# One tile shape per burst of small fp32 matmuls, in a two-layer hybrid encoder trunk on one core

## The chip, the cores and the metric

The kernel runs on one core of one Trainium2 chip, as one program. The metric is the device time of that program in microseconds, from repeated runs. The profiled execution is one more run, recorded instruction by instruction. An engine's name is used as in the profile: PE is TensorE's matmul, PEld its weight load, DVE is VectorE, ACT is ScalarE, POOL is GpSimd, SP issues the DMAs.

## What is computed

Two encoder layers over 256 grid tokens and 16 learned meta tokens (272 rows in all) of width 2048, in float32. Each layer, cut to what matters:

```python
proj = h @ w_in            # 6176 columns: GLA q,k,v,gate,decay and NA q,k,v
y_gla = gla_mixer(...)     # 4 heads, dk 128, dv 256, both directions
y_na  = na_mixer(...)      # 16 heads of 64, windows of 4 x 16 tokens plus the meta tokens
h = layer_norm(ALPHA*h + concat(y_gla, y_na) @ w_out)
h = layer_norm(ALPHA*h + square(relu(h @ w_ff1)) @ w_ff2)
```

In the neighbourhood attention (NA) a grid token attends to its window and the 16 meta tokens, with a learned bias; meta tokens attend to meta tokens alone. The gated linear attention (GLA) is, for each head, a matrix of decayed scores between all tokens, times v. The output is the grid tokens' rows, so the second layer needs no meta rows of its queries and outputs (`full` is false there, and rows are 256 instead of 272).

## The kernel before, in words

Activations lie transposed, features on the 128 partitions and tokens along the free axis, each as a pair of fp32r numbers (high and low part). Weights stream from HBM in tiles of 128x1024; ACT makes the high part (`wh`, L147) and DVE the low part (`wl`, L148). Every large product is three fp32r matmuls per 128x128 block, wh*xh, wh*xl, wl*xh (`three`, L151: L160, L161 and L162 for 272 columns, L156 and L157 for 256; `by_k`, L186). These are the stream that PE works through from end to end.

The mixers' work is much smaller and is written as Python generators: one per GLA head (`gla_head`, L436) in a background queue `bg`, one per pair of NA heads (`na_pair`, L584) in a foreground queue `fg`. `by_m` (L190) calls `pump` after every eighth block row, and `pump` takes one step, that is up to the next `yield`, of the head of `fg` and, by a running credit (GLA_R, GLA_NA), of `bg`. So what one step issues stands on PE as a **burst** between two runs of the large matmuls, about 3 us apart. The framework's scheduler decides the last details of the order on each engine. Bursts are plain fp32, which PE runs as two passes with two weight loads; transposes are one pass.

The steps of a GLA head: nine levels (`order`, L480). For each level POOL makes differences of the cumulated decays (L458) in a tile `lev` of two planes, ACT takes exp (L463), DVE multiplies by q and k (L464); then PE makes the 64x64 blocks of scores (L493: four matmuls of 128 rows x 64 columns, in two column halves) or, at level 8, two 128x128 ones (L488). In the first layer, levels 0 to 4 add the meta tokens' own 16x16 block (L496, 16 weight columns). Then come the scores between meta and grid tokens (L518, 16 weight columns and 256 moving ones; L521 in the first layer), the products with v (L536 to L538), the norm and the gate.

The steps of a pair of NA heads:

1. Scores of 128 queries x 176 keys for two token halves and two heads (L595: 64 rows, the head size), bias added by DVE (L598), softmax (L576 to L582).
2. First layer only: the meta queries' scores (L607, 16 weight columns), mask (L608) and softmax.
3. Transposes of v (L613, L614) and copies into v1 and v2 (L617, L620). v2 holds the values of the keys beyond the first 128, both heads in blocks on the diagonal. In the second layer an empty step follows.
4. Transposes of the probabilities (L630, L631), copied by ACT (L632) and DVE (L633).
5. First layer: transpose of the meta probabilities (L637, 16 rows) and its copy (L639). Then the products with the values: for each token half one 128x128 matmul with v2 (L643) and two of 128x64 with v1 (L645), and in the first layer L647 for the meta queries; then the split into y.

Of the kernel before, what the change touches and what calls it, by code (L numbers as in the profile page):

```python
# [19 lines left out]
L = T + NM  # L20
DEPTH = 2
ROWS, GW = 4, 64
GH, GDK, GDV = 4, 128, 256
# [24 lines left out]
class Trunk:  # L48
# [306 lines left out]
            self.nc.vector.tensor_copy(b[:, 0:1], total)  # L355

    def ev_q(self, m, ps):
        self.nc.scalar.mul(self.qk[m][:, 0, :self.n], ps, GDK ** -0.5)

    def ev_k(self, m, ps, **how):  # L360
        self.nc.scalar.activation(self.qk[m][:, 1, :], ps, AF.Identity, **how)

    def ev_v(self, c, ps):
        vt = self.ep.tile([P, L], F32, name="ft", tag="ft", bufs=4)
# [16 lines left out]
    def ev_na(self, j, ps):  # L381

        nc, m = self.nc, j % 3
        src = ps[:, :T].rearrange("p (r t w) -> p t r w", t=2, r=ROWS)
        if m == 0:
            t = self.a2.tile([P, L], F32, name="nq", tag="nq")
            nc.scalar.mul(t[:, :T].rearrange("p (t r w) -> p t r w", t=2, r=ROWS), src, NAD ** -0.5)
            if self.full:
                nc.vector.tensor_scalar(t[:, T:], ps[:, T:], NAD ** -0.5, None, ALU.mult)
            self.nqkv = [t]  # L390
            return
        if m == 1:
            t = self.a2.tile([P, 2, NKEY], F32, name="nk", tag="nk")
            own, rest = t[:, :, :P], t[:, :, P:]
        else:
            t = own, rest = self.nv[j // 3 % 2]
        nc.scalar.copy(own.rearrange("p t (r w) -> p t r w", r=ROWS), src)
        nc.vector.tensor_copy(rest[:, :, 32:NK2], ps[:, None, T:L].to_broadcast([P, 2, NM]))
        grid = lambda a: a.rearrange("p (r w) -> p r w", r=ROWS)
        for h, lo in ((0, 0), (1, 24)):  # L400
            nc.gpsimd.tensor_copy(grid(rest[:, h, :32]), grid(own[:, 1 - h, :])[:, :, lo:lo + 8])
# [34 lines left out]
    def gla_head(self, h):  # L436
# [5 lines left out]
        Am = g2.tile([NM, L], F32, name="Am", tag="Am")  # L442
        level = lambda: g2.tile([P, 2, L], F32, name="lev", tag="lev", bufs=3)

        def operands(lv):
            if lv == 0:
                q2 = level()[:, 0, :]
                nc.gpsimd.tensor_scalar(q2[:, :n], qk[:, 0, :n], 2.0, 0.0, ALU.mult, ALU.add)
                return q2, qk[:, 1, :]
            w = L if full and lv <= 4 else T  # L450
            B, hb = 1 << lv, 1 << (lv - 1)
            nb = w // B
            t = level()
            v = lambda a: a[:, :w].rearrange("p (b h) -> p b h", h=B)
            f, e, tq, tk = v(bf), v(eb), v(t[:, 0, :]), v(t[:, 1, :])
            mf = f[:, :, hb - 1:hb].to_broadcast([P, nb, hb])
            me = e[:, :, hb:hb + 1].to_broadcast([P, nb, hb])
            tt = lambda o, x, y: nc.gpsimd.tensor_tensor(o, x, y, ALU.subtract)  # L458
            tt(tq[:, :, hb:], f[:, :, hb:], mf)
            tt(tq[:, :, :hb], me, e[:, :, :hb])  # L460
            tt(tk[:, :, :hb], mf, f[:, :, :hb])
            tt(tk[:, :, hb:], e[:, :, hb:], me)
            nc.scalar.activation(t[:, :, :w], t[:, :, :w], AF.Exp, scale=1 / TAU)  # L463
            nc.vector.tensor_tensor(t[:, :, :w], t[:, :, :w], qk[:, :, :w], ALU.mult)  # L464
            return t[:, 0, :], t[:, 1, :]

        def across():
            t = level()
            bm, e0 = bf[:, L - 1:L], eb[:, 0:1]
            ts = nc.gpsimd.tensor_scalar  # L470
            ts(t[:, 0, :T], bf[:, :T], bm, 1.0, ALU.subtract, ALU.mult)
            ts(t[:, 1, T:L], bf[:, T:L], bm, -1.0, ALU.subtract, ALU.mult)
            ts(t[:, 0, T:L], eb[:, T:L], e0, -1.0, ALU.subtract, ALU.mult)
            ts(t[:, 1, :T], eb[:, :T], e0, 1.0, ALU.subtract, ALU.mult)
            nc.scalar.activation(t, t, AF.Exp, scale=1 / TAU)
            nc.vector.tensor_tensor(t[:, 0, :n], t[:, 0, :n], qk[:, 0, :n], ALU.mult)
            nc.vector.tensor_tensor(t[:, 1, :], t[:, 1, :], qk[:, 1, :], ALU.mult)
            return t

        order = (7, 0, 1, 2, 3, 4, 5, 6, 8)  # L480
# [1 line left out]
        for at, lv in enumerate(order):  # L482
# [10 lines left out]
                    nc.tensor.matmul(ps[b * 64:b * 64 + 64, s * 64:s * 64 + 64], lhsT=k[:, c:c + 64],  # L493
                                     rhs=q[:, r:r + 64], start=True, stop=True)
            if full and lv <= 4:
                nc.tensor.matmul(ps[:NM, T:L], lhsT=k[:, T:L], rhs=q[:, T:L], start=True, stop=True)  # L496
# [18 lines left out]
            yield  # L515
        t = ahead
        ps = self.bank()
        nc.tensor.matmul(ps[:NM, :T], lhsT=t[:, 1, T:L], rhs=t[:, 0, :T], start=True, stop=True)  # L518
        if full:
            for s in range(2):  # L520
                nc.tensor.matmul(ps[:, T + s * NM:T + s * NM + NM], lhsT=t[:, 1, s * P:s * P + P],  # L521
                                 rhs=t[:, 0, T:L], start=True, stop=True)
# [37 lines left out]
    def na_tiles(self):  # L560

        def t(name, *shape):
            a = self.a2.tile(list(shape), F32, name=name, tag=name, bufs=1)
            self.nc.gpsimd.memset(a, 0.0)
            return a

        self.nv = [(self.a2.tile([P, 2, P], F32, name=f"nv{i}", tag=f"nv{i}", bufs=1), t(f"nr{i}", P, 2, 64))
                   for i in range(2)]
        self.npr = [t(f"npr{i}", P, 4, 64) for i in range(2)]
        self.nv2 = [t(f"nv2{i}", P, 2, P) for i in range(2)]  # L570
        if self.full:
            self.nms = [t(f"nms{i}", NM, 2, 64) for i in range(2)]

    def softmax(self, s, st, u, outs):
        nc = self.nc
# [8 lines left out]
    def na_pair(self, c, q, k, v):  # L584
# [7 lines left out]
        ps = [self.bank() for _ in range(2)]  # L592
        for t in range(2):
            for hh, hs in enumerate(heads):
                nc.tensor.matmul(ps[hh][:, t * NKEY:t * NKEY + NKEY], lhsT=q[hs, t * P:t * P + P], rhs=k[hs, t, :],  # L595
                                 start=True, stop=True)
        for hh in range(2):
            nc.vector.tensor_tensor(s[:, hh:4:2, :], two(ps[hh][:, :2 * NKEY]), bias[:, 2 * hh:2 * hh + 2, :], ALU.add)  # L598
        pr = self.npr[c % 2]
        self.softmax(s, st, 4, ((s[:, :, :P], s[:, :, :P]), (pr[:, :, :NK2], s[:, :, P:])))  # L600
        yield
        if self.full:
            sm = self.nms[c % 2]
            mt = b.tile([NM, 6], F32, name="mst", tag="mst")
            for hh, hs in enumerate(heads):
                ps = self.bank()
                nc.tensor.matmul(ps[:NM, :NK2], lhsT=q[hs, T:L], rhs=k[hs, 0, P:], start=True, stop=True)  # L607
                nc.vector.tensor_tensor(sm[:, hh, :NK2], ps[:NM, :NK2], self.qmask, ALU.add)  # L608
            self.softmax(sm[:, :, :NK2], mt, 2, ((sm[:, :, :NK2],) * 2,))
            yield  # L610
        pv = self.bank()
        for t in range(2):
            nc.tensor.transpose(pv[:, t * P:t * P + P], v[0][:, t, :], self.ident)  # L613
# [6 lines left out]
                nc.vector.tensor_copy(v2[hh * 64:hh * 64 + NK2, t, hs],  # L620
                                      pv[t * 64:t * 64 + NK2, T + hh * NAD:T + hh * NAD + NAD])
        yield
        if not self.full:
            yield
        p1 = b.tile([P, 4, P], F32, name="p1", tag="p1", bufs=1)
        p2 = b.tile([P, 2, P], F32, name="p2", tag="p2", bufs=1)
        for t in range(2):
            pt = self.bank()
            for hh in range(2):
                nc.tensor.transpose(pt[:, hh * P:hh * P + P], s[:, 2 * t + hh, :P], self.ident)  # L630
            nc.tensor.transpose(pt[:, T:T + P], pr[:, 2 * t:2 * t + 2, :].rearrange("p u c -> p (u c)"), self.ident)  # L631
            nc.scalar.copy(p1[:, 2 * t:2 * t + 2, :], two(pt[:, :T]))  # L632
            nc.vector.tensor_copy(p2[:, t, :], pt[:, T:T + P])  # L633
        yield
        if self.full:
            pt = self.bank()
            nc.tensor.transpose(pt[:, :NM], sm.rearrange("p u c -> p (u c)"), self.ident[:NM, :NM])  # L637
            pm = b.tile([P, NM], F32, name="pm", tag="pm")
            nc.vector.tensor_copy(pm, pt[:, :NM])  # L639
        po = self.bank()  # L640
        for t in range(2):
            r = po[:, t * P:t * P + P]
            nc.tensor.matmul(r, lhsT=v2[:, t, :], rhs=p2[:, t, :], start=True, stop=False)  # L643
            for hh, hs in enumerate(heads):
                nc.tensor.matmul(r[hs], lhsT=v1[:, t, hs], rhs=p1[:, 2 * t + hh, :], start=False, stop=True)  # L645
        if self.full:
            nc.tensor.matmul(po[:, T:L], lhsT=v2[:, 0, :], rhs=pm, start=True, stop=True)  # L647
# [365 lines left out]
```

## Time and profile before

| | us |
|---|---|
| median of 3 runs (lowest, highest) | 2437.83 (2437.68, 2437.95) |
| the profiled execution, whole | 2437.55 |
| its span, first to last instruction | 2435.6 |
| PE busy | 2407.7 (99%) |
| PEld busy | 2260.2 (93%) |
| DVE busy | 1574.8 (65%) |
| ACT busy | 1191.6 (49%) |
| POOL busy | 279.9 (11%) |

The granted clock of TensorE is 0.997 of full speed over the span. The DMA engines move 171 GB/s on average and are busy for about half of the time. The mixers of the first layer lie at about 110 to 390 us, those of the second at about 1350 to 1615 us. In a page of the profile, a group of PE rows reads: line, engine, operation, output<-inputs, tile (weight rows*weight columns), moving shape, count. Lengths of matmuls are modelled and overlap; their starts are what can be compared.

### The profile page before, as it was taken

The numbers are of one execution on the slowest core, as the hardware profiler recorded it, in microseconds if no ns is written. First come the engines' busy times: TensorE is split into PE (matmuls) and PEld (weight loads), VectorE is DVE, ScalarE is ACT, GpSimd is POOL, SyncE is SP. The second block draws the span as 40 slices with busy tenths as digits, with TensorE's granted clock in tenths as the row PEclk, the third lists the DMA queues.
The fourth block names the chain that finished last, engine by engine and source line by source line (L and its number), as shares of the span: only waits on it lengthen the run. The fifth ranks groups of instructions, "written<-read, shape, count | busy, mean of one in ns | idle before, by whom it ended". The sixth has DMA issues, their size and how long they took to land.

```text
span 2435.6 us, 43411 instructions
## 1 busy us (share of the span) xinstructions
PE 2407.7 (99%) x17452; PEld 2260.2 (93%) x17452; DVE 1574.8 (65%) x2481; ACT 1191.6 (49%) x1978; POOL 279.9 (11%) x447
## 2 busy tenths in 40 slices
PE   9999999999999999999999999999999999999997
PEld 9999899999999999999999889898988888888886
DVE  6677777785544455546577787778866555666655
ACT  6555555464433344444456555555644333444443
POOL 1164320020000000000020454300200000000000
PEclk9999999999999999999999999999999999999998
DMA  7544444555555555555556445446566566565564
GB/s 239 164 131 149 134 136 156 174 173 174 175 177 176 173 174 175 175 178 174 174 168 185 145 151 152 133 151 198 182 189 187 187 189 190 185 188 189 183 189 130
DMA packets 118361, 417.26 MB, mean 171 GB/s; under 512 B 13388, under 2 KB 16460, under 8 KB 118160
## 3 DMA queue, kind: packets, MB, share of 16 engines
q1 hardware_dynamic: 118160, 414.49, 54.9%
q8 instruction: 137, 2.24, 0.4%
q14 instruction: 64, 0.52, 0.1%
HBM read 412.34 MB, written 2.10 MB: 170 GB/s over the span
## 4 chain that ended last, share of the span: by engine, by line
PE 94%; DVE 2%; POOL 1%; issue 1%; ACT 1%; DMA 0%; SPq 0%; ACTq 0%; POOLq 0%; DVEq 0%
PE mm L156 22%; PE mm L160 17%; PE mm L162 17%; PE mm L161 17%; PE mm L157 11%; PE mm L186 6%; POOL lev L458 1%; PE bg L493 1%; DVE acc L858 1%; DVE wl L148 1%; PE bg L643 0%; PE bg L595 0%; PE bg L645 0%; PE bg L323 0%; PE bg L536 0%
## 5 line engine op out<-in xcount | busy, mean ns | idle before, releaser
L148 DVE TENSOR_TENSOR wl<-raw,wh 128x1024 fp32r<-128x1024 f32 (+1 forms) x772 | 946.0, 1226 | 648.9 <-ACT wh L147 640.5
L147 ACT CAST wh<-raw 128x1024 fp32r<-128x1024 f32 (+1 forms) x772 | 805.5, 1044 | 951.4 <-PE mm L161 405.5
L160 PE MATMUL mm<-x,wh 128*128 128x272 f32 (+2 forms) x2176 | 632.7, 291 | 0.0
L161 PE MATMUL mm<-x,wh 128*128 128x272 f32 (+2 forms) x2176 | 627.8, 288 | 0.0
L162 PE MATMUL mm<-x,wl 128*128 128x272 f32 (+2 forms) x2176 | 627.6, 288 | 0.0
L160 PEld LDWEIGHTS mm<-x,wh 128*128 128x128 f32 x2176 | 412.5, 190 | 4.4 <-issue 1.4
L162 PEld LDWEIGHTS mm<-x,wl 128*128 128x128 f32 x2176 | 410.2, 188 | 0.2
L161 PEld LDWEIGHTS mm<-x,wh 128*128 128x128 f32 x2176 | 409.6, 188 | 0.0
L156 PE MATMUL mm<-x,wh 128*128 128x512 f32 x1152 | 409.4, 397 | 0.0
L157 PE MATMUL mm<-x,wl 128*128 128x256 f32 x1152 | 324.5, 282 | 0.1
L156 PEld LDWEIGHTS mm<-x,wh 128*128 128x128 f32 x1152 | 217.5, 189 | 52.0 <-issue 1.2
L156 PE MATMUL mm<-y,wh 128*128 128x512 f32 x704 | 247.9, 393 | 0.0
L157 PEld LDWEIGHTS mm<-x,wl 128*128 128x128 f32 x1152 | 217.3, 189 | 0.5 <-DVE wl L148 0.4
L162 PE MATMUL mm<-y,wl 128*128 128x272 f32 x704 | 203.1, 288 | 0.0
L160 PE MATMUL mm<-y,wh 128*128 128x272 f32 x704 | 203.1, 288 | 0.0
L161 PE MATMUL mm<-y,wh 128*128 128x272 f32 x704 | 202.7, 288 | 0.0
L157 PE MATMUL mm<-y,wl 128*128 128x256 f32 x704 | 197.5, 281 | 0.5 <-DVE wl L148 0.5
L156 PE MATMUL mm<-u,wh 128*128 128x512 f32 x512 | 180.6, 393 | 0.0
L458 POOL TENSOR_TENSOR lev<-be 128x128 f32<-128x128 f32 (+1 forms) x256 | 154.7, 634 | 121.7 <-PE bg L493 30.5
L156 PEld LDWEIGHTS mm<-y,wh 128*128 128x128 f32 x704 | 131.8, 187 | 29.9
L162 PE MATMUL mm<-u,wl 128*128 128x272 f32 x512 | 147.7, 289 | 0.0
L160 PE MATMUL mm<-u,wh 128*128 128x272 f32 x512 | 147.7, 288 | 0.0
(242 smaller groups left out, 3286.7 us busy)
## 6 DMA issues: line engine op xcount, KB each, us to landing
raw<-in_wff SPq DMA_DIRECT2D x512, 512.0 KB, 3.5
raw<-in_win SPq DMA_DIRECT2D x190, 512.0 KB, 3.6
raw<-in_wout SPq DMA_DIRECT2D x64, 512.0 KB, 3.6
nb<-in_nab SPq DMA_DIRECT2D x16, 352.0 KB, 3.4
out<-acc SPq DMA_DIRECT2D x8, 256.0 KB, 2.2
xraw<-in_xT SPq DMA_DIRECT2D x7, 272.0 KB, 5.5
wraw<-in_wup SPq DMA_DIRECT2D x2, 392.0 KB
raw<-in_win SPq DMA_DIRECT2D x4, 128.0 KB, 3.0
```

What stands on the lines that cost most here:

```text
L147: nc.scalar.copy(wh[:, c], raw[:, c])
L148: self.wl = nc.vector.tensor_tensor(wl[:, c], raw[:, c], wh[:, c].bitcast(F32), ALU.subtract).ins
L156: mm(ps, lhsT=wh[:, c:c + P], rhs=x.both[:, :, :T], start=first, stop=False)
L157: mm(ps[:, T:], lhsT=wl[:, c:c + P], rhs=xh[:, :T], start=False, stop=last)
L160: mm(o, lhsT=wh[:, c:c + P], rhs=xh[:, :n], start=first, stop=False)
L161: mm(o, lhsT=wh[:, c:c + P], rhs=xl[:, :n], start=False, stop=False)
L162: mm(o, lhsT=wl[:, c:c + P], rhs=xh[:, :n], start=False, stop=last)
L186: self.nc.tensor.matmul(ps[m][:, :n], lhsT=parts[p][0][:, c:c + P], rhs=acts[j][parts[p][1]][:, :n], start=j + p == 0, stop=j == nk - 1 an ...
L458: tt = lambda o, x, y: nc.gpsimd.tensor_tensor(o, x, y, ALU.subtract)
L493: nc.tensor.matmul(ps[b * 64:b * 64 + 64, s * 64:s * 64 + 64], lhsT=k[:, c:c + 64], rhs=q[:, r:r + 64], start=True, stop=True)
L858: return self.nc.vector.tensor_tensor(v, v, by[:, None, :].to_broadcast([P, m, n]), alu)
```

## The change

Within a burst, neighbouring matmuls get the same tile shape (rows and columns of the stationary operand):

- Probabilities times values: the 128x128 matmul with v2 becomes two of 128x64, one per head, in the shape of those with v1; the meta queries' product (L647) too.
- L496: 64 weight columns instead of 16 (the 48 more are whatever lies behind, and their results are not read). For this k is plane 0 and q plane 1 of each two-plane tile, so that the columns behind k's last 16 exist.
- L518: 128 weight columns instead of 16, in the same way.
- L607: the meta queries' scores move into step 1, behind L595, with 128 weight columns instead of 16 (so the meta columns stand first in the query tile); their results lie in the same banks as the others, and the mask is added there.
- L637: the transpose of the meta probabilities becomes a full 128x128 one and moves into step 4 (its tile has 128 rows, zeros below the meta rows), with its copy.
- The empty step of the second layer now comes ahead of the transposes of v; the first layer's number of steps stays.

```diff
     def ev_q(self, m, ps):
-        self.nc.scalar.mul(self.qk[m][:, 0, :self.n], ps, GDK ** -0.5)
+        self.nc.scalar.mul(self.qk[m][:, 1, :self.n], ps, GDK ** -0.5)
...
             if full and lv <= 4:
-                nc.tensor.matmul(ps[:NM, T:L], lhsT=k[:, T:L], rhs=q[:, T:L], start=True, stop=True)
+                nc.tensor.matmul(ps[:64, T:L], lhsT=k[:, T:T + 64], rhs=q[:, T:L], start=True, stop=True)
...
-        nc.tensor.matmul(ps[:NM, :T], lhsT=t[:, 1, T:L], rhs=t[:, 0, :T], start=True, stop=True)
+        nc.tensor.matmul(ps[:, :T], lhsT=flat(t)[:, T:T + P], rhs=t[:, 1, :T], start=True, stop=True)
...
-            self.nms = [t(f"nms{i}", NM, 2, 64) for i in range(2)]
+            self.nms = [t(f"nms{i}", P, 2, 64) for i in range(2)]
...
-                nc.tensor.matmul(ps[hh][:, t * NKEY:t * NKEY + NKEY], lhsT=q[hs, t * P:t * P + P], rhs=k[hs, t, :],
+                nc.tensor.matmul(ps[hh][:, t * NKEY:t * NKEY + NKEY], lhsT=q[hs, NM + t * P:NM + t * P + P], rhs=k[hs, t, :],
                                  start=True, stop=True)
+        if self.full:
+            for hh, hs in enumerate(heads):
+                nc.tensor.matmul(ps[hh][:, 2 * NKEY:2 * NKEY + NK2], lhsT=q[hs, :P], rhs=k[hs, 0, P:],
+                                 start=True, stop=True)
+            meta = self.nms[c % 2]
+            sm = meta[:NM, :, :NK2]
         for hh in range(2):
             nc.vector.tensor_tensor(s[:, hh:4:2, :], two(ps[hh][:, :2 * NKEY]), bias[:, 2 * hh:2 * hh + 2, :], ALU.add)
+            if self.full:
+                nc.vector.tensor_tensor(sm[:, hh, :], ps[hh][:NM, 2 * NKEY:2 * NKEY + NK2], self.qmask, ALU.add)
...
         if self.full:
-            sm = self.nms[c % 2]
             mt = b.tile([NM, 6], F32, name="mst", tag="mst")
-            for hh, hs in enumerate(heads):
-                ps = self.bank()
-                nc.tensor.matmul(ps[:NM, :NK2], lhsT=q[hs, T:L], rhs=k[hs, 0, P:], start=True, stop=True)
-                nc.vector.tensor_tensor(sm[:, hh, :NK2], ps[:NM, :NK2], self.qmask, ALU.add)
-            self.softmax(sm[:, :, :NK2], mt, 2, ((sm[:, :, :NK2],) * 2,))
-            yield
+            self.softmax(sm, mt, 2, ((sm, sm),))
+        yield
         pv = self.bank()
...
         yield
-        if not self.full:
-            yield
         p1 = b.tile([P, 4, P], F32, name="p1", tag="p1", bufs=1)
...
             nc.tensor.transpose(pt[:, T:T + P], pr[:, 2 * t:2 * t + 2, :].rearrange("p u c -> p (u c)"), self.ident)
+            if self.full and t:
+                nc.tensor.transpose(pt[:, T + P:], meta.rearrange("p u c -> p (u c)"), self.ident)
             nc.scalar.copy(p1[:, 2 * t:2 * t + 2, :], two(pt[:, :T]))
             nc.vector.tensor_copy(p2[:, t, :], pt[:, T:T + P])
-        yield
         if self.full:
-            pt = self.bank()
-            nc.tensor.transpose(pt[:, :NM], sm.rearrange("p u c -> p (u c)"), self.ident[:NM, :NM])
             pm = b.tile([P, NM], F32, name="pm", tag="pm")
-            nc.vector.tensor_copy(pm, pt[:, :NM])
+            nc.vector.tensor_copy(pm, pt[:, T + P:T + P + NM])
+        yield
         po = self.bank()
         for t in range(2):
             r = po[:, t * P:t * P + P]
-            nc.tensor.matmul(r, lhsT=v2[:, t, :], rhs=p2[:, t, :], start=True, stop=False)
-            for hh, hs in enumerate(heads):
-                nc.tensor.matmul(r[hs], lhsT=v1[:, t, hs], rhs=p1[:, 2 * t + hh, :], start=False, stop=True)
+            for rest in (True, False):
+                for hh, hs in enumerate(heads):
+                    nc.tensor.matmul(r[hs], lhsT=(v2 if rest else v1)[:, t, hs],
+                                     rhs=p2[:, t, :] if rest else p1[:, 2 * t + hh, :],
+                                     start=rest, stop=not rest)
         if self.full:
-            nc.tensor.matmul(po[:, T:L], lhsT=v2[:, 0, :], rhs=pm, start=True, stop=True)
+            for hs in heads:
+                nc.tensor.matmul(po[hs, T:L], lhsT=v2[:, 0, hs], rhs=pm, start=True, stop=True)
```

`flat` lays the two planes of a tile end to end. In the changed kernel the lines are numbered anew: L493 becomes L497, L496 L500, L518 L522, L521 L525, L595 L599, L607 L603, L613 L620, L630 and L631 L635 and L636, L637 L638, L643 and L645 both L650, L647 L655.

More of the change, by code (lines that the diff above doesn't have):

```diff
@@ L357, in ev_q @@
     def ev_q(self, m, ps):
-        self.nc.scalar.mul(self.qk[m][:, 0, :self.n], ps, GDK ** -0.5)
+        self.nc.scalar.mul(self.qk[m][:, 1, :self.n], ps, GDK ** -0.5)
     def ev_k(self, m, ps, **how):
-        self.nc.scalar.activation(self.qk[m][:, 1, :], ps, AF.Identity, **how)
+        self.nc.scalar.activation(self.qk[m][:, 0, :], ps, AF.Identity, **how)
     def ev_v(self, c, ps):
@@ L386, in ev_na @@
             t = self.a2.tile([P, L], F32, name="nq", tag="nq")
-            nc.scalar.mul(t[:, :T].rearrange("p (t r w) -> p t r w", t=2, r=ROWS), src, NAD ** -0.5)
+            nc.scalar.mul(t[:, NM:].rearrange("p (t r w) -> p t r w", t=2, r=ROWS), src, NAD ** -0.5)
             if self.full:
-                nc.vector.tensor_scalar(t[:, T:], ps[:, T:], NAD ** -0.5, None, ALU.mult)
+                nc.vector.tensor_scalar(t[:, :NM], ps[:, T:], NAD ** -0.5, None, ALU.mult)
             self.nqkv = [t]
@@ L443, in gla_head, with flat @@
         level = lambda: g2.tile([P, 2, L], F32, name="lev", tag="lev", bufs=3)
+        def flat(t):
+            return t.rearrange("p a c -> p (a c)")
         def operands(lv):
             if lv == 0:
-                q2 = level()[:, 0, :]
-                nc.gpsimd.tensor_scalar(q2[:, :n], qk[:, 0, :n], 2.0, 0.0, ALU.mult, ALU.add)
-                return q2, qk[:, 1, :]
+                q2 = level()[:, 1, :]
+                nc.gpsimd.tensor_scalar(q2[:, :n], qk[:, 1, :n], 2.0, 0.0, ALU.mult, ALU.add)
+                return q2, flat(qk)
             w = L if full and lv <= 4 else T
@@ L454, in operands @@
             v = lambda a: a[:, :w].rearrange("p (b h) -> p b h", h=B)
-            f, e, tq, tk = v(bf), v(eb), v(t[:, 0, :]), v(t[:, 1, :])
+            f, e, tq, tk = v(bf), v(eb), v(t[:, 1, :]), v(t[:, 0, :])
             mf = f[:, :, hb - 1:hb].to_broadcast([P, nb, hb])
@@ L464, in operands @@
             nc.vector.tensor_tensor(t[:, :, :w], t[:, :, :w], qk[:, :, :w], ALU.mult)
-            return t[:, 0, :], t[:, 1, :]
+            return t[:, 1, :], flat(t)
         def across():
@@ L470, in across @@
             ts = nc.gpsimd.tensor_scalar
[L471 to L474, printed above, removed]
+            ts(t[:, 1, :T], bf[:, :T], bm, 1.0, ALU.subtract, ALU.mult)
+            ts(t[:, 0, T:L], bf[:, T:L], bm, -1.0, ALU.subtract, ALU.mult)
+            ts(t[:, 1, T:L], eb[:, T:L], e0, -1.0, ALU.subtract, ALU.mult)
+            ts(t[:, 0, :T], eb[:, :T], e0, 1.0, ALU.subtract, ALU.mult)
             nc.scalar.activation(t, t, AF.Exp, scale=1 / TAU)
-            nc.vector.tensor_tensor(t[:, 0, :n], t[:, 0, :n], qk[:, 0, :n], ALU.mult)
-            nc.vector.tensor_tensor(t[:, 1, :], t[:, 1, :], qk[:, 1, :], ALU.mult)
+            nc.vector.tensor_tensor(t[:, 1, :n], t[:, 1, :n], qk[:, 1, :n], ALU.mult)
+            nc.vector.tensor_tensor(t[:, 0, :], t[:, 0, :], qk[:, 0, :], ALU.mult)
             return t
@@ L517, in gla_head @@
         ps = self.bank()
-        nc.tensor.matmul(ps[:NM, :T], lhsT=t[:, 1, T:L], rhs=t[:, 0, :T], start=True, stop=True)
+        nc.tensor.matmul(ps[:, :T], lhsT=flat(t)[:, T:T + P], rhs=t[:, 1, :T], start=True, stop=True)
         if full:
             for s in range(2):
-                nc.tensor.matmul(ps[:, T + s * NM:T + s * NM + NM], lhsT=t[:, 1, s * P:s * P + P],
-                                 rhs=t[:, 0, T:L], start=True, stop=True)
+                nc.tensor.matmul(ps[:, T + s * NM:T + s * NM + NM], lhsT=t[:, 0, s * P:s * P + P],
+                                 rhs=t[:, 1, T:L], start=True, stop=True)
             nc.vector.tensor_copy(A[:, 2:6:3, :NM], ps[:, T:T + 2 * NM].rearrange("p (s c) -> p s c", s=2))
@@ L631, in na_pair @@
             nc.tensor.transpose(pt[:, T:T + P], pr[:, 2 * t:2 * t + 2, :].rearrange("p u c -> p (u c)"), self.ident)
+            if self.full and t:
+                nc.tensor.transpose(pt[:, T + P:], meta.rearrange("p u c -> p (u c)"), self.ident)
             nc.scalar.copy(p1[:, 2 * t:2 * t + 2, :], two(pt[:, :T]))
             nc.vector.tensor_copy(p2[:, t, :], pt[:, T:T + P])
+        if self.full:
+            pm = b.tile([P, NM], F32, name="pm", tag="pm")
+            nc.vector.tensor_copy(pm, pt[:, T + P:T + P + NM])
         yield
-        if self.full:
-            pt = self.bank()
-            nc.tensor.transpose(pt[:, :NM], sm.rearrange("p u c -> p (u c)"), self.ident[:NM, :NM])
-            pm = b.tile([P, NM], F32, name="pm", tag="pm")
-            nc.vector.tensor_copy(pm, pt[:, :NM])
         po = self.bank()
```

## The prediction

> **What bounds the kernel now.** First the page's chain of work that ended last, by engine:
>
> ```profile
> PE 94%; DVE 2%; POOL 1%; issue 1%; ACT 1%; DMA 0%; SPq 0%; ACTq 0%; POOLq 0%; DVEq 0%
> ```
>
> TensorE is the bound: 94% of the chain is its own work. A microsecond taken from PE's queue is a microsecond off the end, except where something else feeds the chain. So I priced the mixers' bursts, the small fp32 products that stand between the big fp32r ones (L156 to L162, called main matmuls here). The timeline of PE, cut to four places, shows one of each sort; columns are start, length, engine, line, tile rows*columns, moving shape, count.
>
> ```profile
> 115.12 0.29 PE L162 MATMUL mm<-x,wl 128*128 128x272 f32 x1
> 115.34 0.45 PE L493 MATMUL bg<-lev 128*64 128x64 f32 x8
> 115.72 0.39 PE L160 MATMUL mm<-x,wh 128*128 128x272 f32 x1
> 115.95 0.29 PE L161 MATMUL mm<-x,wh 128*128 128x272 f32 x1
> ```
> ```profile
> 219.81 0.29 PE L162 MATMUL mm<-x,wl 128*128 128x272 f32 x1
> 219.94 0.38 PE L630 MATMUL bg<-ident,ns 128*128 128x128 f32 x2
> ...
> 220.51 0.37 PE L160 MATMUL mm<-x,wh 128*128 128x272 f32 x1
> 220.72 0.29 PE L161 MATMUL mm<-x,wh 128*128 128x272 f32 x1
> ```
> ```profile
> 223.49 0.29 PE L162 MATMUL mm<-x,wl 128*128 128x272 f32 x1
> 223.70 0.45 PE L493 MATMUL bg<-lev 128*64 128x64 f32 x8
> 224.09 0.23 PE L637 MATMUL bg<-ident,nms 16*128 16x16 f32 x1
> 224.25 0.49 PE L643 MATMUL bg<-p,nv 128*128 128x128 f32 x2
> 224.66 0.44 PE L645 MATMUL bg<-p,v 128*64 128x128 f32 x4
> 225.03 0.49 PE L643 MATMUL bg<-p,nv 128*128 128x128 f32 x2
> 225.45 0.44 PE L645 MATMUL bg<-p,v 128*64 128x128 f32 x4
> 225.82 0.40 PE L647 MATMUL bg<-pm,nv 128*128 128x16 f32 x2
> 226.15 0.45 PE L493 MATMUL bg<-lev,qk 128*64 128x64 f32 x8
> 226.53 0.22 PE L496 MATMUL bg<-lev,qk 128*16 128x16 f32 x2
> 226.67 0.39 PE L160 MATMUL mm<-x,wh 128*128 128x272 f32 x1
> 226.90 0.29 PE L161 MATMUL mm<-x,wh 128*128 128x272 f32 x1
> ```
>
> Starts are to be read, since lengths overlap. A main matmul of 272 columns follows its neighbour at 0.125 us. The burst's **price** is start to start, from the main matmul ahead to the second one behind, less two ordinary steps (0.25 us). The four transposes-only rows (128*128, six records at 0.108) cost 220.72 - 219.81 - 0.25 = 0.66 us: nothing but their own 6 x 0.11. The level products (128*64) cost 0.58, of which their streams are four pairs at 0.053 (the records' starts: 0, 0.007, 0.106, 0.113, 0.165, ...: two column halves run side by side) = 0.21; so **a stay in another shape costs about 0.36** for going in, the first weight load and coming out. Every change of shape between two rows of the third timeline costs again.
>
> An fp32 stream of 128 columns takes 0.107 us, by L643's records (second pass 0.108 behind the first where its weights were already in). For the pair L645 the second pass starts 0.161 behind the first = 0.053 weight load + 0.107, so both halves of 128 columns were through in 0.107.
>
> **The change part by part.** Prices below are no-wait prices of such bursts in the trace, worked out as above.
>
> (1) Probabilities times values, 16 pairs of heads. Before, the two token halves take 0.42 + 0.37 each (224.25 to 225.82: 1.57 for eight streams of 0.107 = 0.86). After, L643 becomes two 128x64 matmuls side by side, same streaming, no change of shape: 0.86 + 0.36 = 1.22. Layer 1 (no meta products): price before 1.575 (at 1591.84), so 8 x 0.355 = 2.8. Layer 0: price before with L637 and L647 is 2.16; after, L647 as two 64-column products adds between 0 (hidden) and 0.24 (the two passes' rows of L647: 0.132 + 0.112); two pair loads of 0.053 less the shorter way out make 0.08, nearest to the L493 rows. 2.16 - 1.30 = 0.86, x 8 = 6.9.
>
> (2) Where levels and these products share a burst they now have one shape. Layer 1's L645 to L493 already shows it: 0.103 from start to start against 0.203 from L645 to L643. Two bursts of layer 0 cost 2.64 before and 1.30 + 0.21 = 1.51 after, 0.27 beyond (1); the burst above costs 3.16, and its parts, now split, 1.57 + 0.58: 0.16 beyond. Sum 0.7.
>
> (3) L496, 20 of them: adding one to a burst costs 0.147 now (0.725 against 0.58). Widened to 64 columns it needs no new shape: two loads of 0.053, less 0.046 because 16 columns leave sooner (L496 goes out in 0.106, L493 in 0.152) = 0.06; bounds 0 and 0.147. 17 x 0.09 = 1.5. Three stand between two levels, where the second level then needs no new entry: 1.248 - 0.725 = 0.52 against 0.23 + 0.06, 3 x 0.23 = 0.7. Sum 2.2.
>
> (4) L518, 8 of them: price 0.735. As 128*128 fp32 it streams as long (2 x 0.215; L536's 256-column rows give 0.215 a pass) plus 0.02, as L488's four 128-column passes cost 0.45 in all. 8 x 0.285 = 2.3. Widening the weights from 16 to 128 columns costs nothing while a 0.107 load lies under a 0.215 stream.
>
> (5) L607: alone 0.39 three times, in company 0.18 to 0.38; sum 2.3. In L595's burst, after: a hidden load, a load of 0.107 in view, less a shorter exit, 0.15 each, between 0.05 (streams alone, 48/128 of 0.107) and 0.21 (two loads); 8 x 0.15 = 1.2. Gain 1.1.
>
> (6) L637 becomes a full transpose in the transposes' burst: 8 x 0.109 = 0.9 lost.
>
> The other edits (index order of the pairs, the query's meta columns first) keep sizes and counts on DVE, ACT and POOL; the mask additions only move ahead of the softmax (0.19 us each). The step that waits on the softmax is still 9 us of main matmuls behind it, so they are hidden; uncovered they would be 16 x 0.19 = 3 us. In layer 1 the transposes of v and its copies (L617 0.36, four of L620 at 0.23) go one step, about 3 us, later; they stay ahead of the p step. No DMA is added, and the wait of POOL for L496 falls away with it.
>
> Sum: 2.8 + 6.9 + 0.7 + 2.2 + 2.3 + 1.1 - 0.9 = **15.1 us** of PE, 4.0 of it in layer 1 (2.8, and half of 2.3).
>
> What comes back as waits: in the chain of layer 1's mixers (1350 to 1615 us) POOL's L458 holds 8.1% and issue 4.6%, and PE's own waits there are
>
> ```profile
> PE bg L493 <- DVE lev L464: 1.6, 2, 1.3
> PE bg L643 <- DVE p L633: 0.8, 1, 0.8
> ```
>
> so a quarter of that stretch isn't PE's: I take 1.0 of the 4.0 back. In layer 0's mixers PE's listed waits sum to 0.2 us; I take back 0.4. Net 15.1 - 1.4 = 13.7. The profiled execution took 2437.55 (span 2435.6 and 1.95 around it); 2437.55 - 13.7 = 2423.85, and the median of the runs lies 0.28 above that execution: **2424.1**. Behind the mixers PE is nearly gapless to the end and DMA half idle, so nothing there eats the gain.
>
> The Trainium skill, TensorEngine Tiling, Key Properties, states that a change of tiling mode drains TensorE while a change of tile doesn't. The trace agrees for the fp32 products (0.203 against 0.103 above), but not everywhere: L323's fp32r products alternate 64 and 32 columns at the main matmuls' own 0.125.
>
> **The rivals.**
> A. Weight loads of one burst don't lie under its streams: then a pass pair of 128 columns takes 0.16 rather than 0.107, 16 x 8 x 0.053 = 6.8 us are lost, and 2430.9 comes out. For it: no row of before has more than two such pass pairs in a row. Against: in L645 the second loads start 0.054 after the first, during the first stream, and in L493 four loads lie under streams.
> The Trainium skill, TensorE: Matmul & The Clock Gate, Part 3, has the rule that would do this: loads overlap running matmuls only in another row group, and the halves share theirs. Those L493 records speak against it.
> B. The halves of a long burst run one after the other: each of the 8 pass pairs takes 0.107 more, 16 x 0.86 = 13.7, which eats the gain: 2437.8. Against: L645's 0.161.
> C. The gain is absorbed: layer 1's 4.0 wholly, and 2 of layer 0's 11.1, where ACT is busy for 50 to 55% and DVE for 66 to 77% (busy time by window): 15.1 - 6.0 = 9.1, 2428.7. For it: the POOL chain. Against: PE's few waits.
> D. Slower: L650 comes sooner after the copies of p and takes the wait that the drains hid. The longest such wait is 1.06 us (at 1544, L643 for L633). The place is the head of all 16 bursts; from 13.7/16 = 0.86 us each the change loses; at 1.06 each, 2437.8 - 13.7 + 17.0 = 2441.1. Against: 13 of 16 have no such wait now, and between the p step and this one lie 2.7 to 3 us of main matmuls in both kernels.
> E. The change does not do what it says, since the entry and exit belong to fp32 in narrow shapes whatever stands beside them: only the widening is left, 0.9 + 0.4 + 20 x 0.06 less L637's own 0.3, about +2: 2440. Against: L645 to L493 at 0.103.
>
> **How the numbers follow.** Forecast 0.76 (bounds of the unknown terms, 20 x 0.08 + 8 x 0.16 + 8 x 0.1, about 3.5 either way: 2420.6 to 2427.6), A 0.08, C 0.07, B 0.03, D 0.03, E 0.03. The range goes from 2420.5 to 2431, so as to take in C and A; what is outside is B, D, E and the forecast's own misses. A measurement of this kernel tells about 0.2% (4.9 us) from no change. Faster by more: forecast, A, C = 0.91; within: B, E and a little of D = 0.07; slower: 0.02.
>
> **What would show it.** Right: bursts of L650 that read x16 or more in 128*64 without another shape between, price near 1.2 to 1.3; L522 entered 0.13 after a main matmul; L500 at 0.05 behind L497. Wrong: pass pairs of L650 0.16 or 0.21 apart (A, B); idle time at L650 that ends with DVE or ACT (D); PE's busy time down by 15 while the span falls by less than 10 (C). A span above 2430 means that one of these terms is mis-sized.

## The result and the profile after

The changed kernel takes 2424.98 us (median of 4 runs, 2424.90 to 2425.17) against 2437.76 (2437.33 to 2437.95): 12.8 us less, ratio 0.9948 with a 95% interval of 0.9931 to 0.9965. The forecast was 2424.1, in a range of 2420.5 to 2431. The page of the profiled execution (2424.98 us) begins, with the chain's shares by engine as the last line:

```profile
span 2423.2 us, 43590 instructions
...
PE 2392.5 (99%) x17532; PEld 2259.4 (93%) x17532; DVE 1575.1 (65%) x2481; ACT 1191.2 (49%) x1978; POOL 290.6 (12%) x447
...
PE 93%; DVE 3%; POOL 1%; issue 1%; ACT 1%; DMA 0%; SPq 0%; ACTq 0%; POOLq 0%; DVEq 0%
```

PE executes 80 records more and is busy for 15.2 us less; the other engines execute as many instructions as before (POOL's spans are rough). The span is 12.4 us shorter. The timeline of PE after shows the values' burst that the prediction showed between 223.49 and 226.90 us:

```profile
223.21 0.29 PE L162 MATMUL mm<-x,wl 128*128 128x272 f32 x1
223.49 0.44 PE L650 MATMUL bg<-p,nv 128*64 128x128 f32 x4
223.76 0.39 PE L650 MATMUL bg<-p,v 128*64 128x128 f32 x4
223.97 0.39 PE L650 MATMUL bg<-p,nv 128*64 128x128 f32 x4
224.19 0.39 PE L650 MATMUL bg<-p,v 128*64 128x128 f32 x4
224.41 0.24 PE L655 MATMUL bg<-pm,nv 128*64 128x16 f32 x4
224.50 0.43 PE L497 MATMUL bg<-lev,qk 128*64 128x64 f32 x8
224.76 0.24 PE L500 MATMUL bg<-lev,qk 128*64 128x16 f32 x2
224.93 0.39 PE L160 MATMUL mm<-x,wh 128*128 128x272 f32 x1
225.16 0.29 PE L161 MATMUL mm<-x,wh 128*128 128x272 f32 x1
```

Everything stands in 128*64. Each L650 row is two pass pairs; in the burst the pairs start 0.109 us apart, the time of one stream of 128 columns, so both column halves stream side by side. The burst now costs 225.16 - 223.21 - 0.25 = 1.70 us; with the one level that now stands in the burst ahead (0.58) that makes 2.28, where it was 3.16. (The transpose L637, now L638, went to that burst too, and adds 0.11 there.)

Where the time went is seen best by following the same main matmuls through both traces. Between two fixed ones around layer 0's mixers the stretch took 292.0 us before (102.5 to 394.5) and 284.7 after: 7.4 us less. Around layer 1's it took 288.0 (1340.1 to 1628.1) and 283.2: 4.75 less. Ahead of the two, the changed kernel is 0.4 us later; between them nothing changed, and behind them it gains 0.4. The prediction had 10.7 and 3.0. So the total came close partly because two misses have opposite signs, and PE's waits say where to look. A row names the engine and line that waited and what released it, then us in total, times and the longest. In layer 0's mixers the list had one row before, and has five after:

```profile
PE bg L647 <- DVE pm L639: 0.2, 1, 0.2
```
```profile
PE bg L540 <- ACT Am L528: 1.3, 1, 1.3
PE bg L650 <- DVE p L640: 0.6, 1, 0.6
PE bg L522 <- DVE lev L481: 0.4, 1, 0.4
PE bg L635 <- DVE nv L627: 0.3, 1, 0.3
PE bg L635 <- DVE ns L586: 0.2, 1, 0.2
```

In layer 1's mixers three rows of the list are new, and L643's row of 0.8 us, shown in the prediction, has no successor:

```profile
PE mm L157 <- DVE wl L148: 0.4, 1, 0.4
PE bg L635 <- DVE nv L627: 0.3, 1, 0.3
PE bg L635 <- DVE ns L586: 0.2, 1, 0.2
```

### The profile page after: what moved, and what is told of

Read it like the earlier page. It is cut to its first block, busy times and chain, and to the rows that moved or that the text cites. A ratio compares the mean times of both kernels' runs of the same rounds, so it can differ in the third digit from the quotient of the medians.

```text
span 2423.2 us, 43590 instructions
## 1 busy us (share of the span) xinstructions
PE 2392.5 (99%) x17532; PEld 2259.4 (93%) x17532; DVE 1575.1 (65%) x2481; ACT 1191.2 (49%) x1978; POOL 290.6 (12%) x447
## 4 chain that ended last, share of the span: by engine, by line
PE 93%; DVE 3%; POOL 1%; issue 1%; ACT 1%; DMA 0%; SPq 0%; ACTq 0%; POOLq 0%; DVEq 0%
PE mm L156 22%; PE mm L160 17%; PE mm L162 17%; PE mm L161 17%; PE mm L157 11%; PE mm L186 5%; POOL lev L462 1%; DVE wl L148 1%; PE bg L497 1%; DVE acc L866 1%; PE bg L650 1%; PE bg L599 0%; PE bg L540 0%; PE bg L323 0%; PE bg L541 0%
## 5 line engine op out<-in xcount | busy, mean ns | idle before, releaser
L148 DVE TENSOR_TENSOR wl<-raw,wh 128x1024 fp32r<-128x1024 f32 (+1 forms) x772 | 946.9, 1227 | 656.0 <-ACT wh L147 646.4
L462 POOL TENSOR_TENSOR lev<-be 128x128 f32<-128x128 f32 (+1 forms) x256 | 162.1, 663 | 108.2 <-ACT gt L337 26.9
```

Of the source, the lines that this page charges most:

```text
L148: self.wl = nc.vector.tensor_tensor(wl[:, c], raw[:, c], wh[:, c].bitcast(F32), ALU.subtract).ins
```

## The experiments

Theory 1 going in: a burst's price depends on its shapes alone, so parts add up; the new waits come from the order that the scheduler now chose on ACT, POOL and DVE. Theory 2: layer 0's helper engines can't follow a faster PE, so part of any gain there comes back as waits.

| kernel | median, us | ratio to before (interval) | layer 0, us less | layer 1, us less |
|---|---|---|---|---|
| changed | 2424.98 | 0.9948 (0.9931 to 0.9965) | 7.4 | 4.75 |
| pv_only | 2428.47 | 0.9964 (0.9951 to 0.9977) | 4.7 | 4.1 |
| gla_only | 2435.15 | 0.9992 (0.9982 to 1.0002) | 1.7 | 0.5 |
| meta_only | 2434.77 | 0.9990 (0.9981 to 1.0000) | 1.0 | 1.4 |
| serial_halves | 2425.02 | 0.9950 (0.9935 to 0.9965) | 7.3 | 4.3 |
| near_shapes | 2427.57 | 0.9962 (0.9948 to 0.9976) | 5.0 | 4.1 |
| am_first | 2423.26 | 0.9944 (0.9929 to 0.9959) | 8.9 | 4.7 |
| level7_wide | 2424.35 | 0.9949 (0.9934 to 0.9963) | 8.3 | 4.3 |
| am_level7 | 2422.63 | 0.9941 (0.9926 to 0.9956) | 9.9 | 4.3 |
| light_dve | 2422.46 | 0.9939 (0.9924 to 0.9954) | 8.8 | 5.6 |
| early_v | 2425.33 | 0.9951 (0.9934 to 0.9967) | 7.4 | 4.5 |
| changed, again | 2424.81 | 0.9948 (0.9933 to 0.9963) | 7.35 | 4.8 |

The kernel before took 2437.08 beside the second to fifth, 2436.93 beside the four with a shape or an order changed (near_shapes to am_level7), and 2437.18 beside the last three. The two right columns are taken from one trace each, between the same main matmuls as above; the two traces of the changed kernel agree within 0.05. By their ratios gla_only and meta_only can't be told from the kernel before, nor most of the lower rows from the changed one, so what follows on them rests on the traces.

### The three parts alone

pv_only makes this edit to the kernel before:

```diff
-            nc.tensor.matmul(r, lhsT=v2[:, t, :], rhs=p2[:, t, :], start=True, stop=False)
-            for hh, hs in enumerate(heads):
-                nc.tensor.matmul(r[hs], lhsT=v1[:, t, hs], rhs=p1[:, 2 * t + hh, :], start=False, stop=True)
+            for rest in (True, False):
+                for hh, hs in enumerate(heads):
+                    nc.tensor.matmul(r[hs], lhsT=(v2 if rest else v1)[:, t, hs],
+                                     rhs=p2[:, t, :] if rest else p1[:, 2 * t + hh, :],
+                                     start=rest, stop=not rest)
...
-            nc.tensor.matmul(po[:, T:L], lhsT=v2[:, 0, :], rhs=pm, start=True, stop=True)
+            for hs in heads:
+                nc.tensor.matmul(po[hs, T:L], lhsT=v2[:, 0, hs], rhs=pm, start=True, stop=True)
```

> The kernel before with one edit: probabilities times values as 128x64 pairs (L643, L645 and L647 in one shape); everything else, L637 ahead of them too, stays. Theory 1 (a price per burst that depends on shapes alone, so that parts add up): the burst costs 1.22 us in layer 1 instead of 1.575 and 1.45 to 1.47 in layer 0 instead of 2.16, as L637's own shape still costs its 0.16 there; 8 x 0.355 + 8 x 0.70 = 8.4 us, some 0.5 more where levels share the burst, less up to 1 us of new waits: 2428.3 to 2430. Theory 2 (layer 0's helpers cannot follow a faster PE, so about a third of any gain in layer 0 comes back as waits, in proportion to the gain): 2.8 + 4.0, about 2431, with waits of PE spread over the bursts of layer 0.

gla_only takes from the change the lines of `ev_q`, `ev_k` and `gla_head`:

```diff
-                nc.tensor.matmul(ps[:NM, T:L], lhsT=k[:, T:L], rhs=q[:, T:L], start=True, stop=True)
+                nc.tensor.matmul(ps[:64, T:L], lhsT=k[:, T:T + 64], rhs=q[:, T:L], start=True, stop=True)
...
-        nc.tensor.matmul(ps[:NM, :T], lhsT=t[:, 1, T:L], rhs=t[:, 0, :T], start=True, stop=True)
+        nc.tensor.matmul(ps[:, :T], lhsT=flat(t)[:, T:T + P], rhs=t[:, 1, :T], start=True, stop=True)
```

> The kernel before with the GLA part alone: planes of q and k swapped, L496 with 64 and L518 with 128 weight columns. Theory 1: 17 x 0.075 + 3 x 0.25 + 8 x 0.29 = 4.3 us less PE work, 3.1 of it in layer 0; waits of its own from a changed order on ACT and POOL, or none, whichever way the order falls: 2433.5 to 2434.5. Theory 2: a third of layer 0's 3.1 comes back: 2434.5, again with waits in proportion to what is saved.

meta_only takes the rest: L607 and L637 moved and widened, the empty step moved, with the values' products as before.

```diff
+        if self.full:
+            for hh, hs in enumerate(heads):
+                nc.tensor.matmul(ps[hh][:, 2 * NKEY:2 * NKEY + NK2], lhsT=q[hs, :P], rhs=k[hs, 0, P:],
+                                 start=True, stop=True)
...
+            if self.full and t:
+                nc.tensor.transpose(pt[:, T + P:], meta.rearrange("p u c -> p (u c)"), self.ident)
```

> The kernel before with the meta tokens' moves of the NA part alone: L607 moved behind L595 and widened, L637 a full transpose in the transposes' burst, the empty step of layer 1 moved; probabilities times values in the old shapes. Theory 1: L607's 2.3 us less 8 x 0.15, less 8 x 0.11 for the transposes, and 8 x 0.35 as L643 is entered from a main matmul in its own shape once L637 is gone: 3.0 us, all in layer 0: 2434.8. Theory 2: 2435.8. If moving the meta work alone brings the late copies of Am in front of L536 (a wait of about 1.3 us once in the changed kernel), the order made by this part is the cause of that wait.

The prices came as theory 1 had them: the values' burst at 1.22 us in layer 1 and 1.455 in layer 0 with L637 still ahead; L500 adds 0.07. In pv_only the time is as theory 1 expected too, though PE has new waits for the copy of the meta probabilities there:

```profile
PE bg L650 <- DVE pm L639: 1.1, 2, 0.9
```

gla_only is a miss for both theories: 1.9 us gained (2437.08 to 2435.15) where 2.6 at the least had been expected. In layer 0 its bursts are 3.0 us cheaper (1.8 by L500, 1.2 by L522), 1.7 arrived. At 141 us the wait for the levels' DVE product (L481) takes what the cheaper L518 gave: start to start, 0.41 became 0.71 there. Most of the rest stands at 246 us (0.4), where PE waits for the copies of p and pm, and at 315 (0.2). In layer 1 the four cheaper L522 make 1.2 us, and 0.5 arrived. meta_only's time (2434.77) is what theory 1 said (2434.8), but by luck: the 3.0 us were to come in layer 0, and 1.0 came there and 1.4 in layer 1. It shows waits at 265, 287, 314 and 380 us, the places where the changed kernel has four of its five; at L536 the listed wait is 0.4, not 1.3, so this part's order makes at most some of that one. The layer 0 gains of the three parts add up to the whole (4.7 + 1.7 + 1.0 = 7.4). Those of layer 1 do not (4.1 + 0.5 + 1.4 = 6.0 against 4.75): two parts each take away the same wait, see early_v.

### Is it the shape around them?

near_shapes gives both widened GLA products a width next to that of the shape around them:

```diff
-                nc.tensor.matmul(ps[:64, T:L], lhsT=k[:, T:T + 64], rhs=q[:, T:L], start=True, stop=True)
+                nc.tensor.matmul(ps[:32, T:L], lhsT=k[:, T:T + 32], rhs=q[:, T:L], start=True, stop=True)
...
-        nc.tensor.matmul(ps[:, :T], lhsT=flat(t)[:, T:T + P], rhs=t[:, 1, :T], start=True, stop=True)
+        nc.tensor.matmul(ps[:64, :T], lhsT=flat(t)[:, T:T + 64], rhs=t[:, 1, :T], start=True, stop=True)
```

> The changed kernel with its two widened GLA products made narrower than the shape around them: L500 with 32 weight columns instead of 64, L522 with 64 instead of 128. Theory 1 (only the same tile shape saves the entry and exit): L500 adds 0.15 again instead of 0.07, 20 times, with 0.17 more for each of three pairs in one burst, and L522 costs 0.74 alone instead of 0.45, 8 times: 1.5 + 0.5 + 2.3 = 4.3 us more, some of it where PE waits anyway: 2428 to 2429.3. Rival (it was the very narrow 16 columns that cost, whatever stands around them): 2425.0.

The timeline of PE, first of the changed kernel, then of near_shapes, at the same burst:

```profile
119.28 0.45 PE L497 MATMUL bg<-lev,qk 128*64 128x64 f32 x8
119.56 0.24 PE L500 MATMUL bg<-lev,qk 128*64 128x16 f32 x2
119.73 0.39 PE L160 MATMUL mm<-x,wh 128*128 128x272 f32 x1
```
```profile
119.02 0.45 PE L497 MATMUL bg<-lev,qk 128*64 128x64 f32 x8
119.40 0.23 PE L500 MATMUL bg<-lev,qk 128*32 128x16 f32 x2
119.57 0.39 PE L160 MATMUL mm<-x,wh 128*128 128x272 f32 x1
```

With 64 columns L500 starts 0.28 behind the levels' first matmul and the burst is left 0.45 after its start; with 32 columns, half the weights, it starts 0.38 behind and the burst lasts 0.55. Burst by burst, L500 adds 0.17 instead of 0.07, and L522 alone costs 0.78 instead of 0.44. So it is the same shape that saves, not a less narrow one; rival E of the prediction falls with it. (The time, 2427.57, is a little under theory 1's 2428 to 2429.3.) The Trainium skill, TensorEngine Tiling, Key Properties, has this as the drain at a change of tiling mode, and this run agrees: 0.152 from the last L497 to L500 in another shape, 0.024 to 0.059 in the same one.

The sum is as telling: these prices make 5.2 us, but only 3.0 arrived (2.35 in layer 0, 0.65 in layer 1). The bursts at 142 and 310 us, which waits make 0.67 and 0.69 us longer in the changed kernel, are 0.07 and 0.08 longer here: PE work put back in filled the waits.

### Must the halves be neighbours?

serial_halves turns two loops of the changed kernel round:

```diff
-            for rest in (True, False):
-                for hh, hs in enumerate(heads):
+            for hh, hs in enumerate(heads):
+                for rest in (True, False):
```

> The changed kernel with one edit: in probabilities times values all products of the first head come before those of the second, so that neighbours stand in the same column half. Theory 1 (two matmuls of 64 columns run side by side only as neighbours in different halves): each of the 16 bursts takes 8 passes of 0.107 more, 0.86 us, 13.7 in all: about 2438.7. Rival (TensorE finds the pairs whatever their order, or what the change saved is not in side by side running): about 2425, the same as the changed kernel.

The rival was right. The burst on PE's timeline:

```profile
287.66 0.29 PE L162 MATMUL mm<-x,wl 128*128 128x272 f32 x1
287.88 0.45 PE L650 MATMUL bg<-p,nv 128*64 128x128 f32 x4
288.15 0.39 PE L650 MATMUL bg<-p,v 128*64 128x128 f32 x4
288.36 0.44 PE L650 MATMUL bg<-p,nv 128*64 128x128 f32 x4
288.58 0.44 PE L650 MATMUL bg<-p,v 128*64 128x128 f32 x4
288.80 0.29 PE L655 MATMUL bg<-pm,nv 128*64 128x16 f32 x4
289.02 0.39 PE L160 MATMUL mm<-x,wh 128*128 128x272 f32 x1
289.25 0.29 PE L161 MATMUL mm<-x,wh 128*128 128x272 f32 x1
```

From the main matmul ahead to the second one behind it takes 1.59 us, where the changed kernel's takes 1.55 at the same burst. Record by record, the second head's first matmul, which the program has behind four passes of the first head, starts 0.013 us after the first head's first; then both halves go on with a pass each 0.109. In the second token half they run 0.057 apart, where the changed kernel has 0.006.

### The wait at 262 us: order or pace?

am_first pins one order of the changed kernel:

```diff
-        nc.scalar.copy(Am[:, :T], ps[:NM, :T])
+        self.am = nc.scalar.copy(Am[:, :T], ps[:NM, :T]).ins
...
-            nc.scalar.activation(t[:, :, :w], t[:, :, :w], AF.Exp, scale=1 / TAU)
+            with self.tc.issue_after(self.am) if self.am else ExitStack():
+                nc.scalar.activation(t[:, :, :w], t[:, :, :w], AF.Exp, scale=1 / TAU)
```

> The changed kernel with one order fixed: from the first head's copy of Am (L528) on, ACT's exp of a level is issued behind the Am copy that was traced before it. In the changed kernel PE waits 1.4 us once, at 262 us, for that copy, which stands behind an exp that itself waits 2.5 us for POOL. Theory 1 (that wait comes from the order that the scheduler chose on ACT and POOL, and only from it): the wait goes and nothing takes its place, 1.3 us less: 2423.7. Theory 2 (the helpers are late for a faster PE in any order): the levels are late instead, 2425.

ACT's timeline before L540 in the changed kernel, then in am_first (lines one higher there):

```profile
259.97 0.35 ACT L624 COPY v<-bg 128x256 f32<-128x256 f32 x1
262.85 0.66 ACT L467 ACTIVATE lev<-lev 128x544 f32<-128x544 f32 x1 [2.53 <-POOL lev L462]
263.41 0.34 ACT L528 COPY Am<-bg 16x256 f32<-16x256 f32 x1
```
```profile
259.54 0.36 ACT L625 COPY v<-bg 128x256 f32<-128x256 f32 x1
259.91 0.36 ACT L529 COPY Am<-bg 16x256 f32<-16x256 f32 x1
260.18 0.63 ACT L468 ACTIVATE lev<-lev 128x512 f32<-128x512 f32 x1
260.71 0.84 ACT L214 CAST am<-Am 16x272 fp32r<-16x272 f32 x2
262.62 0.66 ACT L468 ACTIVATE lev<-lev 128x544 f32<-128x544 f32 x1 [1.07 <-POOL lev L462]
```

In the changed kernel ACT idles 2.5 us at a level's exp while the copy behind it could have run. With the copy first, PE's wait is gone, layer 0 is 1.6 us shorter, and nothing takes its place. So this wait is the order's: theory 1.

### The waits that are left

light_dve leaves out the refinement of the GLA heads' inverse square root:

```diff
-        self.newton(rs, ms, self.eps, tn)
+        nc.scalar.activation(rs, ms, AF.Ln, bias=self.eps)
+        nc.scalar.activation(rs, rs, AF.Exp, scale=-0.5)
```

> The changed kernel without the three DVE instructions of the refinement step of the GLA heads' inverse square root (L432 to L434; that step is left out, so the root is ScalarE's own). They stand ahead of the copies of v2 (L627) at 282.9 to 284.6 us, and PE waits 0.47 us for those copies at 284.6 to reuse their bank. Theory 2 as it now stands (the waits that are left in layer 0 are DVE's pace): that wait goes, and little else changes; 0.5 to 1.0 us less: 2424.0 to 2424.5. Theory 1 (the order chosen by the scheduler makes the waits): the wait stays or moves with the order, 2425.0.

PE's waits in its layer 0:

```profile
PE bg L540 <- ACT Am L528: 1.4, 1, 1.4
PE bg L522 <- DVE lev L481: 0.4, 1, 0.4
PE bg L636 <- DVE ns L587: 0.2, 1, 0.2
```

The waits for v2's copies (284 us) and for p's (310 us) are gone, the one made by the order on ACT stays. Layer 0 is 1.4 us shorter, layer 1 0.8: more than either theory expected, as it took two waits of layer 0 and not one. The wait at 284 us is DVE's pace, theory 2: the refinement's three instructions stood ahead of and between the copies of v2, and without them the same copies end 1.9 us sooner, while PE is only 0.6 sooner at that place. For the wait at 310 that isn't shown, since DVE's order differs there. DVE's timeline in the changed kernel, then in light_dve:

```profile
309.52 1.42 DVE L148 TENSOR_TENSOR wl<-raw,wh 128x1024 fp32r<-128x1024 f32 x1
310.87 0.48 DVE L640 COPY p<-bg 128x128 f32<-128x128 f32 x2
```
```profile
307.57 0.56 DVE L641 COPY p<-bg 128x128 f32<-128x128 f32 x2
...
308.40 1.21 DVE L148 TENSOR_TENSOR wl<-raw,wh 128x1024 fp32r<-128x1024 f32 x1
```

In the changed kernel the low part of a weight tile (L148) comes ahead of the copies of p, as it did in the kernel before, where PE came late enough. In light_dve it comes behind them. level7_wide and am_level7 (below) keep the refinement, have light_dve's order here, and no wait either; am_first has the changed kernel's order, and the wait of 0.6. So another order is enough to remove this wait, and how much of it is pace stays open.

early_v undoes the move of layer 1's empty step:

```diff
             self.softmax(sm, mt, 2, ((sm, sm),))
-        yield
+            yield
         pv = self.bank()
...
         yield
+        if not self.full:
+            yield
         p1 = b.tile([P, 4, P], F32, name="p1", tag="p1", bufs=1)
```

> The changed kernel with one edit undone: in layer 1 the transposes of v and their copies come right behind the softmax step again, and the empty step behind them. In the changed kernel PE's 1.06 us wait for the copies of p at 1544 us is gone although PE came there sooner. Theory (the moved step freed DVE and ACT at that place): the wait comes back, 2425.5 to 2426. Rival (it went because PE's shorter bursts and the order on ACT changed together): no wait there, 2425.0 within 0.3.

The wait of 1.06 us at 1544 did not come back, and the time is 2425.33 us against 2424.81 for the changed kernel beside it: the moved step alone isn't what removed it. It is gone in pv_only, meta_only and early_v, and there in gla_only. The traces show where it arose: in the kernel before and in gla_only ACT idles 3.2 us at a level's exp, waiting for POOL, with the copy of p behind it; in the others it idles 1.6 us at most there. What these share, and so why POOL was sooner, stays open.

### A wider shape where the narrow one stands alone

level7_wide, from the changed kernel:

```diff
-                if lv == 8:
+                if lv > 6:
+                    o = s * P if lv == 7 else P - s * P
                     nc.tensor.matmul(ps[:, s * P:s * P + P], lhsT=k[:, s * P:s * P + P],
-                                     rhs=q[:, P - s * P:T - s * P], start=True, stop=True)
+                                     rhs=q[:, o:o + P], start=True, stop=True)
...
-                        copy(A[half[b], 0:5:4, half[1 - b]], p2[half[b]])
+                        copy(A[half[b], 0:5:4, half[1 - b]], ps[half[b], :T].rearrange("p (s c) -> p s c", s=2)[:, :, half[1 - b]])
```

> The changed kernel with level 7's four 128x64 matmuls of each GLA head replaced by two of 128x128 (twice the scores, half of them not read), in the shape of the main matmuls. Theory 1 (price by shape: 0.58 us for the four narrow ones with entry and exit, 0.45 for two full ones without): 8 x 0.13 = 1.0 us less PE work, all of it in bursts where level 7 stands alone: 2424.0. Rival (a full-width fp32 product pays an entry from fp32r too, or twice the streaming decides): 2425.0 or more.

The burst costs 0.45 us instead of 0.58, as priced, though PE streams twice the scores. The time hardly shows it: layer 0 is 0.9 us shorter, where four bursts account for 0.4 and the wait of 0.69 at 310 went (DVE's order again, see above); layer 1 is 0.45 longer, as the gain and more came back as waits. By its ratio it can't be told from the changed kernel.

> Both edits of the two runs before it in one kernel. Theory 1: the sum, 2.3 us less than the changed kernel: 2422.7. Theory 2: no more than the better of the two.

am_level7 has both edits and came out as theory 1 expected. Its ratio of 0.9941 (0.9926 to 0.9956) is the lowest of those that compute everything, though the intervals overlap; its span is 2420.1 us against 2423.2 and 2422.7 of the changed kernel.

> The changed kernel itself once more, on the chip of the two runs beside it, so that they can be compared with it: 12 to 13 us less than the kernel before, with the same waits at 142, 262, 284, 310 and 374 us if they belong to the program and not to one execution.

It took 2424.81 and has the same five waits, each as long within 0.05 us (and all 0.4 us sooner): they belong to the program.

## Why the prediction was right, and where it was not

- **What bounds the kernel**: right. PE's busy time fell by 15.2 us, the time by 12.8.
- **(1) values**: right. L650 with L655 costs 1.29 us (1.30 foretold), without it 1.22 (1.22).
- **(2) sharing a burst**: mis-sized, 0.5 us instead of 0.7; L655, L497 and L500 together in one burst cost 0.1 more than the sum of their parts.
- **(3) L496**: mis-sized. It adds 0.07 rather than 0.06, and the three pairs save 0.25 each where 0.23 + 0.09 had been counted: 1.8 us instead of 2.2.
- **(4) L518**: right, 0.44 for 0.45 foretold; **(5) L607**: right, 0.152 for 0.15; **(6) L637**: right, 0.109 each.
- **Sum**: 6.9 + 0.5 + 1.8 + 1.2 + 1.1 - 0.9 = 10.6 us in layer 0 and 4.0 in layer 1, 14.6 for 15.1 foretold.
- **What comes back as waits**: this step failed in both layers. In layer 0 it was 3.2 us, not 0.4. The bursts priced with and without waiting show 1.4 more at 262 us, 0.7 at 310, 0.5 at 284, 0.5 at 142 and 0.4 at 374, less 0.2 that went: 3.3. I had read the few waits of before as slack. They only showed that the helpers were in time for the old PE, not by how much: the burst of transposes at 288 us cost 0.75 even then, 0.09 more than without a wait (284 us after the change). The 1.4 is of another sort: the new program has another order on ACT, which I had not followed there. In layer 1, where 1.0 had been taken off, waits shrank by 0.75 us in all. The one of 1.06 at 1544 went, with smaller ones, and three new ones, shown above, came. The 1.0 had no sum behind it: the prediction showed two of the five rows of that list (3.4 us in all), and POOL's share of the chain doesn't say what PE waits.
- **Total**: 13.7 foretold, 12.8 measured; terms of -0.5 and -2.8 in layer 0 and +1.75 in layer 1 partly offset each other. That the total came within 1 us is in part luck; what was priced of PE's work was within 0.5 us of 15.1.
- **The rivals**: A and B fall with the pass pairs at 0.109. The Trainium skill, TensorE: Matmul & The Clock Gate, Part 3, states the rule by which A would have come, that weight loads overlap running matmuls only in another row group. It is not borne out here: the loads of L650 start 0.002 us behind the start of a stream of the same rows. C is what happened in layer 0, where 3.2 us of 10.6, a third, came back; it did not happen in layer 1, where I had expected it. (Its busy shares were misread: the windows give DVE 73 to 77% and ACT 53 to 55%, as the last one is 90 us long.) D's wait exists, once, at 0.69 us. E falls with near_shapes.

## What to carry to other kernels

Price small matmuls start to start between the surrounding large ones, and sort them by tile shape: here each stay in a narrow fp32 shape cost 0.36 us beyond its streams (the levels' own streams are 0.21), and widening a product into the shape around it cost 0.07 us instead of 0.15 (L496) and 0.44 instead of 0.735 (L518). Before counting such a gain in full, look how early the helpers are at each burst, not how rarely PE waits; a third of layer 0's gain went there. A change of PE work can change the scheduler's order on other engines, so follow those queues through the new program as well; pinning one order on ACT gave back 1.6 of the 3.2 us that layer 0 had lost.

## What was not expected of the hardware

Matmuls in different column halves of the array didn't need to be neighbours in the program to run side by side: with four passes of the first half ahead of it, a matmul of the second half started 0.013 us after the first of them, and the burst lost 0.04 us. And an fp32 product of twice the size in the full shape took less time in the stream (0.45 us) than the needed half in narrow shapes (0.58).
